# Bank order and operand spacing in the down products, and the order of work in the feed-forward norm

## The chip, the cores and the metric

The kernel runs on one core of a Trainium2 chip. The metric is the device time of one execution in microseconds. The core has five engines with a queue of instructions each, worked off in order: TensorE (PE) multiplies into eight PSUM banks, VectorE (DVE) and ScalarE (ACT) do elementwise work and can read PSUM, GpSimd (POOL) does elementwise work in SBUF and issues DMAs, SyncE (SP) issues DMAs.

## What is computed

Two decoder layers over 1024 tokens of width 1024, float32, each with a mixer, a cross-attention to 256 memory tokens and a feed-forward part. The change touches the last two.

```python
x = x + mixer(rms(x))
x = x + memory_cross_attention(rms(x), rms(mem))
x = x + swiglu(rms(x))

def swiglu(h, w_gate_up, w_down):       # hidden width 2816
    g, u = jnp.split(h @ w_gate_up, 2, axis=-1)
    return (jax.nn.silu(g) * u) @ w_down
```

## The kernel before

The residual `x` stays in SBUF, transposed: 8 blocks of 128 features, each in two halves of 512 tokens. Each float32 product is made of three matmuls (`mm3`): both operands are split in a high half (ScalarE casts, L333 for weights, L134 for operands of the down) and a low half (VectorE subtracts, L334 and L135), and high x high, high x low and low x high are accumulated.

**Seven products for eight.** The feed-forward products are done in a Winograd form: a two by two arrangement of blocks needs seven products of sums of blocks in place of eight. A product is 4 x 3 = 12 matmuls of 128 x 512. The sums of weights (s1 to s4) are made by DMAs that accumulate, issued on GpSimd's queue (L328, `add_to`), in the raw buffers `wraw` (five of them); `plan_sums` plans the loads, `pair_blocks` takes the products in a given order, splits each weight and issues the sums. `prefetch` keeps two weights split ahead of TensorE. The sums of operands (t1 to t4) are made on VectorE.

**The feed-forward loop** (`ffn`). 22 blocks of 128 hidden features. Block 0 is done plainly (`gate_up_plain`, eight products of twelve matmuls), blocks 1 to 21 by `gate_up` with seven products each, in the order of the table `ORDER`. `after` takes a product out of its bank (copies on ScalarE in `new`, L2016; adds on VectorE). `gate` scales by the norm's rows, does the Silu after a set time of the program's own clock, and scales again; `up` multiplies, and gives the hidden tile to `Down.feed`. After every even block from the second on, a down (`Down.out`) of the two blocks before takes place: seven products of four row blocks, each accumulated in a bank of its set (a, b or c, four banks each) and added to or subtracted from `x` by VectorE right after its matmuls (L193). One product's result goes into `x` in two places by letting the bank accumulate: the bank's sum is added, then the next product is put on top of it and the sum is added elsewhere. A matmul into a bank that is in use waits for the add that reads it. There are 10 downs a layer, and one in each cross-attention; the last blocks go through `outproj`.

**Operands of the down** (`Down.build`): for each chunk of two blocks, seven operands are made as soon as the hidden tiles are there: `11`, `t1`, `t2`, `21`, `t3`, `t4`, `22`, each with a cast and a low half, the four sums with a VectorE operation more. They share a number of buffers, of which a product gives its two back.

**The norm before it** (`norm_quarter`). The last products of cross-attention (`outproj`, adds at L671) come by quarters of `x`; after each, the quarter is scaled and split into operands for the gate/up products (L277, L278), squared on ScalarE (L1928) and the squares are added on GpSimd (L1932). The quarter (0, 1) makes the mixed operand t1 (L1958, L1959) and `12`, by a cast and a low half each (L1920, L1921). After the last quarter `rest` makes t2 (L1962), t3 (L1965) and t4 (L1968), and `stats` sums the squares by matmuls (`ssq`), takes the inverse root (L449 to L454) and broadcasts it (`rbp`).

**The order of work.** The program is written by generators (`Threads`) that run against a clock of the program's own, which TensorE's instructions move; a `yield` of a number lets that time pass, of an event waits for it. That fixes the order in which instructions are written down; a scheduler then lays each engine's queue in that order where operands and buffers allow. So a `yield` isn't a wait on the chip, but a place in the queues.

## Time and profile before

| | us |
|---|---|
| median of 3 runs | 2621.82 |
| lowest and highest | 2619.26, 2626.28 |
| profiled execution | 2623.92 |
| its span, first to last instruction | 2622.2 |
| TensorE busy in it | 2500.2 (95%) |
| VectorE busy in it | 1963.2 (75%) |
| ScalarE busy in it | 1079.6 (41%) |
| GpSimd busy in it | 563.0 (21%) |

The profile is of one execution. An engine's busy time is the union of its instructions' bars; a matmul's bar is longer than the interval at which matmuls follow each other, so a busy TensorE isn't one at its peak. A wait is put down to the instruction whose end released the one that waited.

### The profile page before, as it was taken

The numbers are of one execution on the slowest core, as the hardware profiler recorded it, in microseconds if no ns is written. First come the engines' busy times: TensorE is split into PE (matmuls) and PEld (weight loads), VectorE is DVE, ScalarE is ACT, GpSimd is POOL, SyncE is SP. The second block draws the span as 40 slices with busy tenths as digits, with TensorE's granted clock in tenths as the row PEclk, the third lists the DMA queues.
The fourth block names the chain that finished last, engine by engine and source line by source line (L and its number), as shares of the span: only waits on it lengthen the run. The fifth ranks groups of instructions, "written<-read, shape, count | busy, mean of one in ns | idle before, by whom it ended". The sixth has DMA issues, their size and how long they took to land. (4 is left out here: it accounts for less than half of the span.)

```text
span 2622.2 us, 34426 instructions
## 1 busy us (share of the span) xinstructions
PE 2500.2 (95%) x12029; PEld 2021.8 (77%) x12029; DVE 1963.2 (75%) x3717; ACT 1079.6 (41%) x2125; POOL 563.0 (21%) x559
## 2 busy tenths in 40 slices
PE   8999998999999999999999999999899999999998
PEld 7788886777777777779998788788677777777777
DVE  5767779877777777774637788786987777777777
ACT  5323555433333333343323377574543333333333
POOL 5311324111112111140000210032321111211122
PEclk9999999999999999999999999999999999999999
DMA  5232311455555555521122132121145555555553
GB/s 134 56 85 77 92 37 45 97 111 111 112 113 112 113 113 109 113 61 36 41 49 56 37 76 61 49 85 45 44 89 109 109 113 110 112 115 114 113 113 101
DMA packets 300093, 227.32 MB, mean 87 GB/s; under 512 B 28911, under 2 KB 250320, under 8 KB 299920
## 3 DMA queue, kind: packets, MB, share of 16 engines
q1 hardware_dynamic: 226688, 150.28, 19.7%
q0 software_dynamic: 72912, 74.32, 18.4%
q8 instruction: 94, 1.54, 0.2%
q14 instruction: 79, 0.65, 0.1%
q10 hardware_dynamic: 320, 0.53, 0.1%
HBM read 176.84 MB, written 4.19 MB: 69 GB/s over the span
## 5 line engine op out<-in xcount | busy, mean ns | idle before, releaser
L333 ACT CAST whi<-wraw 128x512 fp32r<-128x512 f32 (+1 forms) x652 | 393.0, 616 | 877.1 <-DMA wraw<-wraw 354.1
L334 DVE TENSOR_TENSOR wlo<-wraw,whi 128x512 fp32r<-128x512 f32 (+1 forms) x652 | 460.1, 716 | 223.1 <-ACT whi L333 218.5
L256 PE MATMUL dn<-fh,whi 128*128 128x512 f32 x1456 | 457.0, 401 | 36.7 <-DVE x L193 34.3
L193 DVE TENSOR_TENSOR x<-x,dn 128x512 f32<-128x512 f32 x728 | 457.3, 692 | 0.0
L256 PEld LDWEIGHTS dn<-fh,whi 128*128 128x128 f32 x1456 | 261.4, 188 | 133.6 <-DVE x L193 65.0
L256 PE MATMUL gu<-xth,whi 128*128 128x512 f32 x688 | 272.7, 396 | 18.4 <-ACT f L2016 18.4
L256 PE MATMUL dn<-fh,wlo 128*128 128x512 f32 x728 | 271.3, 394 | 0.0
L256 PE MATMUL gu<-xtl,whi 128*128 128x512 f32 x688 | 270.5, 393 | 0.0
L256 PE MATMUL gu<-xth,wlo 128*128 128x512 f32 x688 | 269.7, 392 | 0.0
L256 PE MATMUL gu<-xgh,wlo 128*128 128x512 f32 x552 | 217.0, 400 | 25.4 <-DVE wlo L334 25.3
L256 PE MATMUL pj<-xgh,whi 128*128 128x512 f32 x592 | 240.4, 406 | 0.0
L256 PE MATMUL pj<-xgh,wlo 128*128 128x512 f32 x592 | 232.6, 395 | 5.1 <-DVE wlo L334 5.1
L256 PE MATMUL pj<-xgl,whi 128*128 128x512 f32 x592 | 232.7, 393 | 0.0
L256 PE MATMUL gu<-xgh,whi 128*128 128x512 f32 x552 | 223.2, 404 | 9.4 <-DVE x L671 9.1
L256 PE MATMUL gu<-xgl,whi 128*128 128x512 f32 x552 | 219.3, 397 | 0.0
L328 POOL DMA_DIRECT2D wraw<-in_ffn_w_gate_up_dram x84 | 109.4, 1302 | 504.9 <-DVE wlo L334 210.2
L328 POOL DMA_DIRECT2D wraw<-wraw x136 | 126.6, 931 | 365.4 <-DMA wraw<-wraw 165.8
L256 PEld LDWEIGHTS gu<-xth,whi 128*128 128x128 f32 x688 | 129.1, 188 | 56.7 <-ACT f L2016 28.3
L134 ACT CAST fh<-f 128x512 fp32r<-128x512 f32 x148 | 89.5, 621 | 173.2 <-DVE f L165 69.6
L256 PEld LDWEIGHTS dn<-fh,wlo 128*128 128x128 f32 x728 | 136.7, 188 | 31.2
L256 PEld LDWEIGHTS gu<-xth,wlo 128*128 128x128 f32 x688 | 129.2, 188 | 29.3
L256 PEld LDWEIGHTS gu<-xtl,whi 128*128 128x128 f32 x688 | 129.2, 188 | 27.8
(494 smaller groups left out, 4855.5 us busy)
## 6 DMA issues: line engine op xcount, KB each, us to landing
wraw<-in_ffn_w_gate_up_dram SPq DMA_DIRECT2D x218, 256.0 KB, 2.9
wraw<-wraw POOLq DMA_DIRECT2D x136, 256.0 KB, 3.3
wraw<-in_ffn_w_down_dram SPq DMA_DIRECT2D x108, 256.0 KB, 2.7
wraw<-in_ffn_w_gate_up_dram POOLq DMA_DIRECT2D x84, 256.0 KB, 5.0
wraw<-in_od_w_in_dram SPq DMA_DIRECT2D x42, 256.0 KB, 2.8
wraw<-in_ffn_w_down_dram POOLq DMA_DIRECT2D x40, 256.0 KB, 4.2
wraw<-in_ev_w_in_dram SPq DMA_DIRECT2D x32, 256.0 KB, 2.6
wraw<-in_xattn_wkv_dram SPq DMA_DIRECT2D x32, 256.0 KB, 2.7
```

Source lines behind the costliest of these rows:

```text
L134: self.t.nc.scalar.copy(hi, src)
L193: getattr(nc.vector, op)(x, x, ps)
L256: self.nc.tensor.matmul(out, lhsT, rhs, start=start, stop=stop, skip_group_check=onto)
L328: return Step(self.th, lambda: self.nc.gpsimd.dma_start(out=raw, in_=src, accum_op=ALU.add), delay, before)
L333: self.nc.scalar.copy(hi, raw)
L334: (eng or self.nc.vector).tensor_sub(lo, raw, hi.bitcast(F32))
```

## The change

In the down products (both in the feed-forward part and in cross-attention), the order of the seven products is changed so that no two products in a row use the same banks: a, b, a, c, a, c, a. The order in which weights are loaded and summed follows the same table. Operand `22` is made before t4. In the feed-forward part a pace of 2400 ns of the program's clock is put between the making of operands, and the operands of a chunk are begun when the down before it has been written down. The unused callbacks by quarters are dropped.

In the feed-forward norm the quarter (0, 1) is split plainly like the others; the squares, their sums (now on VectorE) and the mixed operand t1 come after the last quarter, the squares first, then t1 to t4 with 1500 ns between their tiles. Block 1 of the gate/up products gets an order of its own (`first`) with s1 and s4 ahead of s2. The Silu in `gate` and in block 0 is put later by 800 and 1500 ns of the program's clock.

```diff
--- before.py
+++ after.py
@@ -119,13 +119,15 @@
 
 
 
-    FORM = (("11", "11", "a", 0, 0, 1), ("12", "21", "b", 0, 0, 1), ("s2", "t2", "a", 0, 1, 1), ("s3", "t3", "a", 1, 1, -1),
-            ("22", "t4", "a", 1, 0, -1), ("s1", "t1", "c", 1, 1, -1), ("s4", "22", "c", 0, 1, 1))
-    DONE = {"12": (0, 0), "22": (1, 0), "s1": (1, 1), "s4": (0, 1)}
-
-    def __init__(self, t, tags, eng=None, sign=1):
-        self.t, self.tags, self.eng, self.sign = t, list(tags), eng or t.nc.vector, sign
+    FORM = (("11", "11", "a", 0, 0, 1), ("12", "21", "b", 0, 0, 1), ("s2", "t2", "a", 0, 1, 1), ("s1", "t1", "c", 1, 1, -1),
+            ("s3", "t3", "a", 1, 1, -1), ("s4", "22", "c", 0, 1, 1), ("22", "t4", "a", 1, 0, -1))
+
+    def __init__(self, t, tags, eng=None, sign=1, pace=None):
+
+        self.t, self.tags, self.eng, self.sign, self.pace = t, list(tags), eng or t.nc.vector, sign, pace
         t.th.free[self] = len(self.tags)
+        self.over = {-1: Event()}
+        t.th.set(self.over[-1])
         self.full, self.right, self.ev = {}, {}, {}
 
     def parts(self, src, eng):
@@ -142,6 +144,7 @@
     def feed(self, c, i, h, tile):
         if c not in self.ev:
             self.ev[c] = {nm: Event() for nm in ("11", "21", "22", "t1", "t2", "t3", "t4")}
+            self.over[c] = Event()
             self.t.th.spawn(self.build(c))
         self.full[c, i, h] = tile
 
@@ -154,13 +157,19 @@
                 yield 500
             return self.full[c, i, h]
 
-        def operand(nm, src):
+        def operand(nm, src, fresh=True):
+            if self.pace and fresh:
+                yield self.pace / 2
             yield (self, 2)
             self.right[c, nm] = self.parts(src, self.eng)
             t.th.set(self.ev[c][nm], 2500)
+            if self.pace:
+                yield self.pace / 2 if fresh else self.pace
 
         b11 = yield from tile(0, 0)
-        yield from operand("11", b11)
+        if self.pace:
+            yield self.over[c - 1]
+        yield from operand("11", b11, False)
         b12 = yield from tile(0, 1)
         t.nc.vector.tensor_sub(b11, b11, b12)
         yield from operand("t1", b11)
@@ -168,14 +177,14 @@
         t.nc.vector.scalar_tensor_tensor(b11, b11, -1.0, b22, op0=ALU.mult, op1=ALU.subtract)
         yield from operand("t2", b11)
         b21 = yield from tile(1, 0)
-        yield from operand("21", b21)
+        yield from operand("21", b21, False)
         t.nc.vector.tensor_sub(b12, b22, b12)
         yield from operand("t3", b12)
+        yield from operand("22", b22, False)
         t.nc.vector.scalar_tensor_tensor(b11, b11, -1.0, b21, op0=ALU.mult, op1=ALU.subtract)
         yield from operand("t4", b11)
-        yield from operand("22", b22)
-
-    def out(self, c, on_quarter=None):
+
+    def out(self, c):
         t, nc, banks = self.t, self.t.nc, {}
         for w, r, to, i, h, sign in self.FORM:
             hi, lo = t.block()
@@ -194,8 +203,7 @@
                 if m % 2:
                     yield 0
             self.give(mine)
-            if on_quarter is not None and w in self.DONE:
-                on_quarter(*self.DONE[w])
+        t.th.set(self.over[c])
 
 
 class Norm:
@@ -1885,12 +1893,13 @@
         self.plan_rows(wd, (FB - 2) * P)
 
     ORDER = {"mid": (("11", "11"), ("12", "21"), ("s2", "t2"), ("s1", "t1"), ("s3", "t3"), ("s4", "22"), ("22", "t4")),
+             "first": (("11", "11"), ("12", "21"), ("s1", "t1"), ("s4", "22"), ("s2", "t2"), ("s3", "t3"), ("22", "t4")),
              "last": (("11", "11"), ("12", "21"), ("s2", "t2"), ("s1", "t1"), ("s3", "t3"), ("22", "t4"), ("s4", "22"))}
     BANK = {"11": "a", "12": "b", "s2": "a", "s1": "c", "s3": "a", "s4": "c", "22": "a"}
 
     @classmethod
     def order(cls, j):
-        return cls.ORDER["last" if j == FB - 1 else "mid"]
+        return cls.ORDER["last" if j == FB - 1 else "first" if j == 1 else "mid"]
 
     def norm_quarter(self, N, gname, off):
 
@@ -1902,51 +1911,48 @@
         N.free12 = Event()
         x, g = self.xT, [self.gain(gname, off + k) for k in range(KB)]
         ng = [self.neg[:, off + k:off + k + 1] for k in range(KB)]
-        accs, t, b12 = [[], []], [None] * 4, [None] * 4
+        accs, t, b12 = [None] * 2, [None] * 4, [None] * 4
 
         def plain(nm, i, h):
             B[nm] = []
+            tag = "g" if nm == "12" else "xg"
             for k in range(4 * i, 4 * i + 4):
-                hi, lo = self.g("xg", dt=F32R, name="xgh"), self.g("xg", dt=F32R, name="xgl")
+                hi, lo = self.g(tag, dt=F32R, name="xgh"), self.g(tag, dt=F32R, name="xgl")
                 self.split(x[h][k], hi, lo, g[k])
                 B[nm].append((hi, lo))
             th.set(N.b_ev[nm], 2000)
 
-        def mixed(nm, tag, srcs, make, eng):
+        def mixed(nm, tag, srcs, make):
             B[nm] = []
             for k in range(4):
                 make(k)
                 hi, lo = self.g(tag, dt=F32R, name="xth"), self.g(tag, dt=F32R, name="xtl")
-                nc.scalar.copy(hi, srcs[k])
-                eng.tensor_sub(lo, srcs[k], hi.bitcast(F32))
+                self.split(srcs[k], hi, lo)
                 B[nm].append((hi, lo))
-            th.set(N.b_ev[nm], 2000)
-
-        def squares(i, h, some=4):
-            for k in range(4 * i, 4 * i + 4):
-                sq = self.g("p" if k % 2 else "pt", name="sq")
-                nc.scalar.activation(sq, x[h][k], AF.Square)
-                if len(accs[h]) == 0 or k % 4 >= some:
-                    accs[h].append(sq)
-                else:
-                    nc.gpsimd.tensor_add(accs[h][0], accs[h][0], sq)
+                yield 1500
+            th.set(N.b_ev[nm], 500)
 
         def stats():
-            yield 500
-            squares(1, 1)
-            yield 4000
+            for h in range(NH):
+                for k in range(KB):
+                    sq = self.g("p", name="sq")
+                    nc.scalar.activation(sq, x[h][k], AF.Square)
+                    if k == 0:
+                        accs[h] = sq
+                    else:
+                        nc.vector.tensor_add(accs[h], accs[h], sq)
+                    yield 750
             ps = self.ps("ssq")
+            yield 1500
             self.col_sums(ps[:, 0:4], accs[0], stop=False)
-            yield 5000
             self.col_sums(ps[:, 4:8], accs[1], start=False)
-            cols = self.g("pt", (P, 3, 8), name="ncols")
+            cols = self.g("p", (P, 3, 8), name="ncols")
             v, y, tmp = (cols[:, n, :] for n in range(3))
             nc.vector.tensor_scalar(v, ps[:, 0:8], 1.0 / D, EPS, op0=ALU.mult, op1=ALU.add)
             self.rsqrt(v, y, tmp)
             for h in range(NH):
                 N.col[h] = y[:, 4 * h:4 * h + 4]
-                th.set(N.col_ev[h], 8000)
-            yield N.col_ev[0]
+            yield 5500
             for h in range(NH):
                 psb = self.bcast_cols(N.col[h], "rbp")
                 N.rb[h] = self.g("rb", name="rb")
@@ -1954,7 +1960,7 @@
                 th.set(N.rb_ev[h], 0)
 
         def t1(k):
-            b12[k], t[k] = self.g("g", name="b12"), self.g("p", name="bt")
+            b12[k], t[k] = self.g("g", name="b12"), self.g("pt", name="bt")
             nc.scalar.activation(b12[k], x[1][k], AF.Identity, scale=g[k])
             nc.vector.scalar_tensor_tensor(t[k], x[0][k], g[k], b12[k], op0=ALU.mult, op1=ALU.subtract)
 
@@ -1968,24 +1974,22 @@
             nc.vector.scalar_tensor_tensor(t[k], x[0][4 + k], ng[4 + k], t[k], op0=ALU.mult, op1=ALU.subtract)
 
         def run(i, h):
-            if (i, h) == (0, 1):
-                mixed("t1", "o", t, t1, nc.vector)
-                mixed("12", "g", b12, lambda k: None, nc.vector)
-            else:
-                plain(f"{i + 1}{h + 1}", i, h)
+            plain(f"{i + 1}{h + 1}", i, h)
             if (i, h) == (1, 1):
                 th.spawn(rest())
-                th.spawn(stats())
-                return
-            squares(i, h)
 
         def rest():
-            yield 2000
-            mixed("t2", "xg", t, t2, nc.vector)
-            yield 2500
-            mixed("t3", "g", b12, t3, nc.vector)
+            yield 1000
+            yield from stats_first()
+            yield from mixed("t1", "o", t, t1)
+            yield from mixed("t2", "xg", t, t2)
+            yield from mixed("t3", "g", b12, t3)
             yield N.free12
-            mixed("t4", "g", t, t4, nc.vector)
+            yield from mixed("t4", "g", t, t4)
+
+        def stats_first():
+            th.spawn(stats())
+            yield 12000
 
         return run
 
@@ -1993,7 +1997,7 @@
         nc, th = self.nc, self.th
         last = FB // 2 - 1
         hid, hid_ev = [[None, None], [None, None]], [Event(), Event()]
-        down = Down(self, ["pt"] * 4 + ["g"] * 4 + ["r"] * self.BUFS["r"], nc.vector, sign=-1)
+        down = Down(self, ["pt"] * 4 + ["g"] * 4 + ["r"] * self.BUFS["r"], nc.vector, -1, 2400)
 
         def hidden(j, h, t):
 
@@ -2008,7 +2012,7 @@
         def gate_up(j):
 
 
-            last = j == FB - 1
+            start, last = j == 1, j == FB - 1
             bank, t, done = {}, {}, {}
 
             def new(nm, ps):
@@ -2018,7 +2022,7 @@
             def gate(h, g):
                 yield N.rb_ev[h]
                 nc.vector.tensor_mul(g, g, N.rb[h])
-                yield 2000
+                yield 2800
                 nc.scalar.activation(g, g, AF.Silu)
                 yield 900
                 nc.vector.tensor_mul(g, g, N.rb[h])
@@ -2037,14 +2041,21 @@
                 elif w == "12":
                     nc.vector.tensor_add(t["p"], t["p"], ps)
                     th.spawn(gate(0, t["p"]))
+                elif w == "s2" and start:
+                    nc.vector.tensor_add(t["u"], t["u"], ps)
+                    th.spawn(gate(1, t["u"]))
                 elif w == "s2":
                     new("u", ps)
                 elif w == "s1":
                     new("v", ps)
                 elif w == "s3":
                     nc.vector.tensor_add(t["v"], t["v"], ps)
+                    if start:
+                        th.spawn(up(1, t["v"], t["v"]))
                     if last:
                         new("w", ps)
+                elif w == "s4" and start:
+                    new("u", ps)
                 elif w == "s4":
                     nc.vector.tensor_add(t["u"], t["u"], ps)
                     th.spawn(gate(1, t["u"]))
@@ -2075,6 +2086,7 @@
                 yield N.rb_ev[h]
                 t = self.g("p", name="f")
                 nc.vector.tensor_mul(t, gp, N.rb[h])
+                yield 1500
                 nc.scalar.activation(t, t, AF.Silu)
                 yield 1200
                 nc.vector.scalar_tensor_tensor(t, t, -1.0, up, op0=ALU.mult, op1=ALU.mult)
```

## Rows read from the trace of the kernel before

**Rows 1.** The page: the span, TensorE's busy time, and two lines of the view in 40 equal slices (tenths of busy time, tenths of full clock).

```profile
span 2622.2 us, 34426 instructions
...
PE 2500.2 (95%) x12029; PEld 2021.8 (77%) x12029; DVE 1963.2 (75%) x3717; ACT 1079.6 (41%) x2125; POOL 563.0 (21%) x559
...
PE   8999998999999999999999999999899999999998
...
PEclk9999999999999999999999999999999999999999
```

**Rows 2.** What TensorE waited for over the whole span: who waits, for whom, us in total, times, longest.

```profile
PE dn L256 <- DVE x L193: 34.3, 50, 1.7
PE gu L256 <- DVE wlo L334: 25.3, 23, 2.4
PE gu L256 <- ACT f L2016: 18.4, 23, 2.9
PE gu L256 <- DVE x L671: 9.1, 2, 4.6
```

**Rows 3.** Busy time by stretches (start:end, length, then busy us and number of instructions for PE, PEld, DVE, ACT and POOL, granted clock, DMA share, GB/s). The first two are the feed-forward layers from the first down to the last products, the other two what lies before, from the norm on.

```profile
515.30:1128.30 613.00, 580.31 (x2437) 448.93 (x2436) 465.39 (x758) 208.04 (x366) 114.80 (x113) 1.00 0.54 112
1966.75:2579.45 612.70, 580.36 (x2437) 448.81 (x2436) 465.41 (x758) 208.87 (x367) 116.19 (x115) 1.00 0.53 112
434.69:515.30 80.61, 69.86 (x289) 55.27 (x289) 68.38 (x107) 39.52 (x68) 25.74 (x22) 0.92 0.36 79
1886.20:1966.75 80.55, 69.75 (x289) 55.34 (x289) 68.30 (x106) 38.88 (x67) 25.52 (x21) 0.92 0.37 79
```

**Rows 4.** A stretch of gate/up products in the chain of work that ended last: start, length, number of matmuls.

```profile
2499.29 28.42 PE gu L256 x124
```

**Rows 5.** The same view by stretches of one cycle: a down with its tail, and the two gate/up blocks after it.

```profile
642.58:668.40 25.82, 22.75 (x92) 16.30 (x91) 24.14 (x41) 6.33 (x11) 4.35 (x4) 1.00 0.46 92
668.40:706.42 38.02, 37.20 (x162) 30.15 (x161) 23.85 (x39) 15.32 (x28) 7.85 (x8) 1.00 0.59 125
```

**Rows 6.** VectorE's order of time in that down: start, length, operation, number in a row, and in brackets the idle time before it and what ended it.

```profile
643.56 0.69 DVE L334 TENSOR_TENSOR wlo<-wraw,whi 128x512 fp32r<-128x512 f32 x1 [2.86 <-ACT whi L333]
...
646.76 1.28 DVE L193 TENSOR_TENSOR x<-x,dn 128x512 f32<-128x512 f32 x2
...
667.72 2.50 DVE L193 TENSOR_TENSOR x<-x,dn 128x512 f32<-128x512 f32 x4
```

**Rows 7.** VectorE's groups in that down, 643.5 to 668.35: busy us, mean ns, idle time before.

```profile
L135 DVE TENSOR_TENSOR fh<-f,fh 128x512 fp32r<-128x512 f32 x3 | 2.1, 694 | 0.0
```

**Rows 8.** TensorE in order of time, in the same down and at its end.

```profile
651.79 2.43 PE L256 MATMUL dn<-fh,whi 128*128 128x512 f32 x8 [0.73 <-DVE x L193]
...
655.29 0.73 PE L256 MATMUL dn<-fh,whi 128*128 128x512 f32 x2 [1.07 <-DVE x L193]
...
664.88 0.50 PE L256 MATMUL gu<-xgh,wlo 128*128 128x512 f32 x1 [1.00 <-DVE wlo L334]
```

**Rows 9.** ScalarE's copy out of a bank in the second gate/up block after it, and TensorE's matmul that waits for it.

```profile
697.40 0.57 ACT L2016 COPY f<-gu 128x512 f32<-128x512 f32 x1
...
698.02 0.50 PE L256 MATMUL gu<-xth,whi 128*128 128x512 f32 x1 [0.82 <-ACT f L2016]
```

**Rows 10.** The accumulating transfer for a gate/up weight as it is issued on GpSimd's queue, and ScalarE's cast of that weight (the first of three).

```profile
665.13 0.89 POOL L328 DMA_DIRECT2D wraw<-wraw  x1 [2.11 <-DVE wlo L334]
...
668.72 1.88 ACT L333 CAST whi<-wraw 128x512 fp32r<-128x512 f32 x3 [8.88 <-DMA wraw<-wraw]
```

**Rows 11.** Stretches at the feed-forward norm of the first layer, as in rows 3, and TensorE's first gate/up matmul there.

```profile
434.50:439.40 4.90, 0.35 (x2) 0.01 (x1) 4.90 (x5) 1.20 (x4) 3.46 (x3) 1.00 0.00 0
...
439.40:452.00 12.60, 9.95 (x27) 6.97 (x28) 12.60 (x16) 8.22 (x15) 7.90 (x6) 0.59 0.15 43
452.00:474.00 22.00, 21.04 (x99) 16.91 (x97) 22.00 (x39) 9.63 (x17) 6.66 (x6) 1.00 0.25 48
...
439.42 0.52 PE L256 MATMUL gu<-xgh,whi 128*128 128x512 f32 x1 [4.57 <-DVE x L671]
```

**Rows 12.** VectorE at that norm: low halves in order of time, then its groups from 434.5 to 477.5, and GpSimd's adds of squares from 416 to 477.5 (busy us, mean ns).

```profile
419.05 0.76 DVE L278 SCALAR_TENSOR_TENSOR xgl<-x,gains,xgh 128x512 fp32r<-128x512 f32 x1
...
420.32 1.80 DVE L278 SCALAR_TENSOR_TENSOR xgl<-x,gains,xgh 128x512 fp32r<-128x512 f32 x1
...
476.76 0.68 DVE L1921 TENSOR_TENSOR xtl<-bt,xth 128x512 fp32r<-128x512 f32 x1
...
L334 DVE TENSOR_TENSOR wlo<-wraw,whi 128x512 fp32r<-128x512 f32 x8 | 8.7, 1088 | 0.0
L278 DVE SCALAR_TENSOR_TENSOR xgl<-x,gains,xgh 128x512 fp32r<-128x512 f32 x8 | 8.2, 1024 | 0.0
L1921 DVE TENSOR_TENSOR xtl<-bt,xth 128x512 fp32r<-128x512 f32 x9 | 7.2, 802 | 0.5 <-ACT xth L1920 0.5
L1921 DVE TENSOR_TENSOR xtl<-b,xth 128x512 fp32r<-128x512 f32 x7 | 6.9, 990 | 0.0
L1962 DVE SCALAR_TENSOR_TENSOR bt<-x,neg,bt 128x512 f32<-128x512 f32 x4 | 4.0, 1000 | 0.0
...
L1932 POOL TENSOR_TENSOR sq<-sq 128x512 f32<-128x512 f32 x14 | 23.7, 1696 | 31.8 <-ACT sq L1928 31.0
```

**Rows 13.** A stretch of cross-attention with its down, as in rows 3.

```profile
390.00:402.50 12.50, 11.84 (x58) 8.99 (x57) 11.54 (x25) 8.22 (x19) 2.83 (x3) 1.00 0.06 22
```

## The prediction

> **What bounds the kernel now.** I read first the page's busy line and its forty slices: TensorE is busy 2500.2 of 2622.2 us and sits at 8 or 9 tenths nearly everywhere, at a clock of 9 tenths or more [rows 1]. So time can only come from TensorE's own gaps. Second, the list of what TensorE waited for: of about 122 us, 34.3 go to matmuls of the down products (`dn`) waiting for VectorE's residual adds (L193), 25.3 to gate/up matmuls (`gu`) waiting for a weight's low half (L334), 18.4 to `gu` waiting for ScalarE's copy out of a bank (L2016), 9.1 to two waits of 4.6 us for L671 [rows 2]. All lie in the two feed-forward layers, so third, these by stretches.
>
> Idle time understates a wait, as a matmul's bar outlasts its issue interval. 124 undisturbed matmuls of `gu` take 28.42 us, 0.229 each [rows 4]. From the first down to the last products a layer has 10 downs of 84 and 19 gate/up blocks of 84 matmuls: 2436 x 0.229 = 557.8 us, and takes 613.0 and 612.7 [rows 3]. **Excess: 55 us a layer, 5.5 us for each of 20 downs.** The stretch before it, from the norm through gate/up blocks 0 to 2, has 264 long matmuls (60.5 us) and 24 short ones, which I put at 0.1 each, 2.5: 63.0, and takes 80.6 [rows 3], **17.6 us too much, twice**. These 145 us are the most that the change can reach.
>
> In one cycle the down and its tail last 25.8 us with VectorE busy 24.1 of them, the two gate/up blocks 38.0 with VectorE busy 23.9 [rows 5]. VectorE is the limit in the down alone. Its queue there runs without a hole from the first adds on, one operation each 0.60 us (four in 2.50, the last lasting 0.70) [rows 6]. A product gives it 4 adds and one low half, 5 x 0.60 = 3.0 us, while TensorE needs 12 x 0.229 = 2.75. Also in that queue are gate operations, low halves of operands (L135, three) and one operand sum [rows 6, 7]. TensorE waits 0.73 and 1.07 us where a product returns to the bank of the product just before it [rows 8], which leaves the adds only one product's time.
>
> **The change, part by part.**
>
> *Bank order in the down.* The same 84 matmuls and 28 adds; banks go a, b, a, c, a, c, a instead of a, b, a, a, a, c, c. A bank then rests for a whole product between uses. I walk the queue from a down's start (642.6) with the first add where it is now, 646.76 or +4.2 [rows 6]: ahead of it lie a low half that waits 2.86 us for its cast, and gate operations. With 0.60 an operation and the first add of the third product done at about +12.0, the fifth product, due at 4 x 2.75 = +11.0, waits 1.0; the sixth and seventh another 0.25 each, as VectorE loses 0.25 to 0.3 a product; three restarts, which I put at 0.1 each. Sum 1.8 us. If the later Silu (2.8 instead of 2 us in the program's own time) lets adds go first and they begin 0.7 earlier, it is 0.6 or less. The planner takes the weights' order from the same table, so s1 is read fourth instead of sixth and frees its raw buffer sooner. No DMA is added: each set keeps four accumulating transfers on GpSimd's queue and five loads on SP's; the new order equals that of the gate/up blocks, which run at 0.229 in rows [rows 4]. So I cost it at nothing; without that cover a late transfer costs TensorE its own 3.6 us, from the issue to the cast (665.13 to 668.72) [rows 10].
>
> *Spacing of operands.* Building the seven operands now spreads over 2.4 us steps, and those of the next chunk wait for the end of the present down. That takes three operations (one sum, two low halves) out of the down's queue, 43 to 40, and 1.8 us of VectorE into the next gate/up block, which has 38.0 - 23.9 = 14 us to spare per two blocks [rows 5]. It also ends the bunch after the odd block, where ScalarE's copy at 697.40 came behind casts of operands and TensorE waited 0.82 [rows 9]. Nothing is queued behind a wait that didn't exist; the last operand, t4, needs buffers that the first product frees, 2.75 us into the down, and is wanted 16.5 us in. Cost zero, covered by 14 us. Behind TensorE's gate/up wait for a low half (1.00 at 664.88 [rows 8]) stood the adds; now that low half is queued before the adds of the last two products and TensorE comes first by less than 1 us, if at all.
>
> *Remainder of a cycle:* 1.8 for banks, 0.5 for what is left of the other waits and their restarts, 2.3 of 5.5. **Gain 3.2 x 20 = 64 us**; from 0.6 + 0.2 left (4.7 x 20 = 94) down to 1.5 x 20 = 30, if weights become late (first rival).
>
> *Feed-forward norm.* Before, TensorE stands still at 434.5 for 4.57 us [rows 11], since the banks it wants wait for adds that stand behind mixed operands and low halves on VectorE. The half-filled stretch after that idle time runs at a granted clock of 0.59, that is mostly at the lower of the two levels, 1.2 GHz; then the clock is back at 1.00 [rows 11]. While GpSimd adds squares (14 of 1.70 us) VectorE's low halves take 1.80 instead of 0.76, eight of them 1.02 on average [rows 12]. After, the quarter has 4 low halves in place of 12 operations, no GpSimd add runs, and TensorE should start the gate/up products almost at once: 4.6 + the next waits + the slow clock, together most of the 16.6 us that remain of 17.6 when 1.0 is left to block 2.
>
> What it adds comes later. VectorE gets 14 adds of squares (8.4 us at 0.60) and the 8 operations of t1 (5.0). Its queue is full from 434.5 to 474 [rows 11], the last low half of t4 beginning at 476.76 [rows 12], 42.9 us after the start. From this go 9.6 us of stretched time (sum over groups of the excess over 0.69 and 0.74), 7.4 that now run before the start, and 13.4 come on: 39.3. But TensorE is earlier, so 16 operations (evacuations, adds, gates, two weights) get in before: 9.6, in all 48.9. TensorE wants the last t4 tile 43 us after the start (22.0 for block 0, 2.5 short ones, 6 products and a part of block 1). So it waits about 6, with restarts and a part of t3 7.5. **Gain 9 a layer, 18**; from 16 (the 16 operations stay behind) to 4 (a second slow stretch of 12.6 us at 0.59, worth 12.6 x 0.41 = 5.2 [rows 11]). The new order of block 1 wants s4 fourth: two chained transfers within four products, hidden by block 0; a miss costs up to 3.6 once a layer. Squares on ScalarE move by 16 x 0.62; it is busy 9.6 of 22 us there [rows 11].
>
> *Cross-attention* uses the new bank order unpaced. Banks a and c stay occupied from the fourth product on, where a was freed after the fifth. TensorE there is busy 11.84 of 12.5 us [rows 13], attention being nearly through by then: between -1 and +3 us a layer; I take 0.
>
> **Sum:** 64 + 18 = 82 us off a span of 2622.2, 2540.2. The profiled execution took 2623.92 with 1.7 around its span; the median of the runs, 2621.82, is 2.1 below that. So 2540.2 + 1.7 - 2.1 = 2539.8, **2540 us**.
>
> **Rivals.** *Late weights* take the place of the bank wait. The third gate/up weight is the first one plus another, accumulated in place: its cast began 3.6 us after that issue [rows 10], then its own low half. Now it is ready about 2 us before use; with TensorE ahead, by my walk (first low half done +20.5, cast +24.4, low half done +26.4, wanted +26.6) 0.2. VectorE also carries 40 + 20 operations, 36 us, in a down and the next block of 38.4. If low halves lag 2.5 us more, 20 x 2.5 = 50 are lost: 2590, between 2568 and 2615. For it: the 2.86 us hole before a low half [rows 6]. Against it: weights precede adds in the queue.
>
> *The alternation has no effect*: c must take over b's banks, and if these are late, products four to seven wait as before. Left are the norm, 18, and about 1 us a cycle of copies: 2584. Against it: b gets the whole third product's time.
>
> *t4 comes last* (slower). Its low half is issued within the down. If it were queued behind the adds, it would end at VectorE's end, about +25.7, instead of before +18.3. TensorE would wait 7.4 a down, 4.2 more than the 3.2 gained: 2622 + 84 - 18 = 2688. It decides from some +21.5 on, when the wait eats the gain. Against it: it can start at about +5, some 13 us early.
>
> *The clock falls in the downs* (slower). Granted clock was 1.00 with all bank waits [rows 3] and 0.59 after 4.57 us of standing still. A stretch like that one, 5.2 us, in each down would add 104: 2644. Nothing in rows of downs shows it. The Trainium skill, TensorE: Matmul & The Clock Gate, section A second HAM failure mode: psum-queue depth-cycling, speaks for it: it tells of a kernel that cycled through banks each iteration, idled briefly between groups and so swung between half and full clock. By that rule shorter but more frequent holes would be worse; the trace so far disagrees, with 50 bank waits at 1.00.
>
> **Chances.** Forecast (2505 to 2568) 0.62; better still 0.05; late weights 0.17; no alternation 0.06; t4 0.06; clock 0.04. A measurement tells about 0.3%, 8 us, from no change. Of late weights 0.04 and of no alternation 0.01 fall within it. Faster 0.62 + 0.05 + 0.13 + 0.05 = 0.85, same 0.05, slower 0.10. The range 2505 to 2595 holds 0.62 + 0.11 + 0.05 = 0.78.
>
> **What would show it.** Right: waits of `dn` for L193 fall from 34.3 to under 15 us; those for L2016 under 5; a cycle of some 60 us with VectorE's busy share up to 80%; no 4.6 us hole at the norm and a clock near 1.00 there, but `gu` waits on L1921 in block 1. Wrong: `gu` waits for L334 above 25 us, or dn cycles still of 62 us or more; or a clock under 0.9 in downs.

## The result, and the profile after

The changed kernel took 2550.95 us (median of 4 runs, 2543.97 to 2555.85) beside 2622.55 for the kernel before (4 runs, 2619.26 to 2626.28): ratio 0.9725, 95% interval 0.9704 to 0.9746, faster by 71.6 us. The forecast was 2540, from 2505 to 2595.

The page of the kernel after, against [rows 1]: the span is 70.6 us shorter, TensorE has the same 12029 matmuls, and its clock stays at 9 tenths or more.

```profile
span 2551.6 us, 34493 instructions
...
PE 2475.9 (97%) x12029; PEld 2028.3 (79%) x12029; DVE 1953.1 (77%) x3745; ACT 1077.7 (42%) x2125; POOL 518.1 (20%) x531
...
PEclk9999999999999999999999999999999999999999
```

What TensorE waited for, after (who, for whom, us in total, times, longest). L2020 is the copy that was L2016, L202 the residual add that was L193, L341 and L342 the weight's cast and low half that were L333 and L334:

```profile
PE gu L264 <- ACT f L2020: 21.3, 20, 2.5
...
PE dn L264 <- DVE x L202: 5.1, 13, 0.6
PE dn L264 <- ACT whi L341: 3.4, 6, 0.6
...
PE gu L264 <- DVE f L2045: 2.6, 2, 1.4
```

Against [rows 2], the waits of the down fell from 34.3 to 5.1, those for a weight's low half (25.3) and for L671 (9.1) are gone, and those for ScalarE's copy grew from 18.4 to 21.3.

Where the time came from, by the same stretches as [rows 3] (one cycle first, then the two steady stretches, then the two norm stretches; columns as there):

```profile
627.05:687.00 59.95, 58.45 (x253) 47.16 (x253) 46.70 (x78) 21.60 (x38) 11.69 (x12) 1.00 0.57 119
502.75:1090.55 587.80, 570.56 (x2432) 454.15 (x2432) 463.44 (x758) 207.32 (x367) 115.63 (x113) 1.00 0.56 117
1922.85:2508.75 585.90, 572.33 (x2432) 451.75 (x2432) 463.22 (x758) 207.41 (x367) 116.80 (x115) 1.00 0.56 117
432.25:502.75 70.50, 66.21 (x295) 52.83 (x294) 66.35 (x118) 39.99 (x71) 9.96 (x10) 1.00 0.40 84
1849.95:1922.85 72.90, 69.25 (x295) 55.13 (x294) 66.59 (x118) 40.19 (x71) 9.96 (x10) 0.95 0.39 83
```

The steady stretches give 25.2 and 26.8, **52.0 us** (64 forecast); the norm stretches 10.1 and 7.7, **17.8** (18 forecast); the rest of the span 0.8 (0 forecast). The cycle shown is one of the best: the eight from the second to the last down of layer 0 take 486.0, 60.7 each.

What is left in a cycle, in VectorE's order of time, kernel after (start, length, idle time before and what ended it):

```profile
600.80 0.69 DVE L2060 TENSOR_TENSOR f<-f,gu 128x512 f32<-128x512 f32 x1 [1.41 <-PE gu L264]
605.88 0.69 DVE L342 TENSOR_TENSOR wlo<-wraw,whi 128x512 fp32r<-128x512 f32 x1 [4.39 <-ACT whi L341]
606.49 0.68 DVE L2024 TENSOR_TENSOR f<-f,rb 128x512 f32<-128x512 f32 x1
607.87 0.69 DVE L2028 TENSOR_TENSOR f<-f,rb 128x512 f32<-128x512 f32 x1 [0.70 <-ACT f L2026]
608.48 0.68 DVE L2035 TENSOR_TENSOR f<-gu,f 128x512 f32<-128x512 f32 x1
...
609.68 0.69 DVE L2035 TENSOR_TENSOR f<-f 128x512 f32<-128x512 f32 x1
```

And ScalarE's in the same stretch:

```profile
605.22 0.62 ACT L341 CAST whi<-wraw 128x512 fp32r<-128x512 f32 x1 [6.75 <-DMA wraw<-wraw]
607.20 0.63 ACT L2026 ACTIVATE f<-f 128x512 f32<-128x512 f32 x1 [1.36 <-DVE f L2024]
...
609.20 0.62 ACT L136 CAST fh<-f 128x512 fp32r<-128x512 f32 x1 [0.85 <-DVE f L2035]
610.39 0.62 ACT L136 CAST fh<-f 128x512 fp32r<-128x512 f32 x1 [0.58 <-DVE f L2035]
610.92 0.58 ACT L2020 COPY f<-gu 128x512 f32<-128x512 f32 x1
```

**The held-up gate.** The weight s2 is the first weight with s1 added, and s1 is itself a sum. The accumulating DMA that makes s2 is issued by GpSimd at 601.27, after 4.67 us of waiting for the one that makes s1. So ScalarE's cast is preceded by 6.75 idle us and VectorE's low half by 4.39. Behind that low half stands the gate's scaling (L2024), whose input L2060 was done at 601.5. From there everything goes in a row: Silu, scaling, hidden tiles, the operands' casts, and behind those in ScalarE's queue (at 610.92) the copy out of the bank that TensorE wants. TensorE waits 2.53 at 611.55 (row below). The same hole before a down makes its first add late, as it did in the kernel before (2.86 us [rows 6]).

### The profile page after: what moved, and what is told of

It is laid out like the page before. It is cut to its first block, busy times and chain, and to the rows that moved or that the text cites. A ratio compares the mean times of both kernels' runs of the same rounds, so it can differ in the third digit from the quotient of the medians.

```text
span 2551.6 us, 34493 instructions
## 1 busy us (share of the span) xinstructions
PE 2475.9 (97%) x12029; PEld 2028.3 (79%) x12029; DVE 1953.1 (77%) x3745; ACT 1077.7 (42%) x2125; POOL 518.1 (20%) x531
## 3 DMA queue, kind: packets, MB, share of 16 engines
q8 instruction: 95, 1.56, 0.3%
## 4 chain that ended last, share of the span: by engine, by line
PE 53%; DVE 13%; DMA 8%; issue 4%; ACT 2%; POOL 0%; DVEq 0%; ACTq 0%; POOLq 0%
PE gu L264 17%; PE dn L264 12%; PE pj L264 6%; PE tp L264 4%; PE op L264 4%; DMA wraw<-wraw 4%; DVE wlo L342 3%; DMA wraw<-in_ffn_w_gate_up_dram 3%; DVE x L202 3%; PE as L264 2%; PE ao L264 1%; PE apt L268 1%; DMA wraw<-in_ffn_w_down_dram 1%; ACT whi L341 1%; DVE f L2024 1%
## 5 line engine op out<-in xcount | busy, mean ns | idle before, releaser
L341 ACT CAST whi<-wraw 128x512 fp32r<-128x512 f32 (+1 forms) x652 | 397.5, 616 | 931.7 <-DMA wraw<-wraw 304.6
L342 DVE TENSOR_TENSOR wlo<-wraw,whi 128x512 fp32r<-128x512 f32 (+1 forms) x652 | 449.7, 695 | 198.8 <-ACT whi L341 194.0
L202 DVE TENSOR_TENSOR x<-x,dn 128x512 f32<-128x512 f32 x728 | 451.4, 676 | 0.0
L264 PEld LDWEIGHTS dn<-fh,whi 128*128 128x128 f32 x1456 | 267.4, 188 | 91.7 <-issue 19.5
L264 PE MATMUL gu<-xth,whi 128*128 128x512 f32 x672 | 268.2, 399 | 27.0 <-ACT f L2020 21.3
L264 PE MATMUL dn<-fh,wlo 128*128 128x512 f32 x728 | 285.4, 393 | 0.0
L336 POOL DMA_DIRECT2D wraw<-in_ffn_w_gate_up_dram x84 | 116.2, 1383 | 527.0 <-DVE wlo L342 255.2
L264 PE MATMUL gu<-xgh,wlo 128*128 128x512 f32 x568 | 222.2, 391 | 0.0
L264 PEld LDWEIGHTS pj<-xgh,wlo 128*128 128x128 f32 x592 | 112.2, 190 | 31.2 <-DVE wlo L342 7.2
```

Source lines behind the costliest of these rows:

```text
L202: getattr(nc.vector, op)(x, x, ps)
L264: self.nc.tensor.matmul(out, lhsT, rhs, start=start, stop=stop, skip_group_check=onto)
L336: return Step(self.th, lambda: self.nc.gpsimd.dma_start(out=raw, in_=src, accum_op=ALU.add), delay, before)
L341: self.nc.scalar.copy(hi, raw)
L342: (eng or self.nc.vector).tensor_sub(lo, raw, hi.bitcast(F32))
```

## Experiments

Each ratio is to the kernel before on the same chip. "At 2622.5" is the ratio times 2622.55, so that runs can be compared; differences between runs in us are taken from the ratios in this way.

**Parts of the change alone.** *e1_banks*: before, with the new order of banks and weights only.

```diff
-    FORM = ... s2/a, s3/a, 22/a, s1/c, s4/c
+    FORM = ... s2/a, s1/c, s3/a, s4/c, 22/a
-        (operand 22 after t4)
+        (operand 22 before t4)
```

> The kernel before with the new order of the seven down products alone (and operand 22 built before t4); no spacing of operands, nothing of the norm. Theory (banks are the main part of the cycle's gain, 5.5 us of excess a cycle to about 3): waits of dn for the residual adds fall from 34 to under 15 us and the time by 35 to 60 us, to 2563 to 2588. Rival (VectorE's queue, not the bank, sets the down, and the new order pays only together with spaced operands): waits move to gu waiting for low halves, time within 15 us of before, 2608 to 2622.

Measured 2628.56, ratio 0.999 (0.9979 to 1.0000). **Alone, the bank order gains nothing that can be told**, as the rival said, but the waits did not move to low halves. Those fell from 25.3 to 5.4 us, while the copy's grew from 18.4 to 31.5, and those of `dn` became shorter and more (kernel e1_banks, waits as above):

```profile
PE dn L256 <- DVE x L193: 42.2, 74, 0.8
PE gu L256 <- ACT f L2016: 31.5, 21, 2.9
...
PE gu L256 <- DVE wlo L334: 5.4, 4, 2.4
```

VectorE's order of time before a down of that kernel shows one reason. The hole ahead of the s2 low half is 3.59 us, and the first add comes 4.9 after the down's start (643.29), where it was 2.86 and +4.2 [rows 6]; over all 20 downs the mean of that hole goes from 2.5 to 3.4 and the mean first add from +3.8 to +4.7.

```profile
645.00 0.69 DVE L334 TENSOR_TENSOR wlo<-wraw,whi 128x512 fp32r<-128x512 f32 x1 [3.59 <-ACT whi L333]
645.61 0.68 DVE L2020 TENSOR_TENSOR f<-f,rb 128x512 f32<-128x512 f32 x1
...
648.20 1.28 DVE L193 TENSOR_TENSOR x<-x,dn 128x512 f32<-128x512 f32 x2
```

*e3_norm*: the norm part with block 1's order and block 0's later Silu, without the rest.

```diff
 (after)
-    FORM = new;  22 before t4;  Down(..., -1, 2400);  gate: yield 2800
+    FORM = old;  22 after t4;   Down(..., -1);        gate: yield 2000
```

> The kernel before with the changed feed-forward norm, the order of block 1 and the later Silu in block 0 alone; old bank order, no spacing, the old time of the gate's Silu. Theory (the norm's part stands by itself): the stretch from the norm to the first down gets 8 to 10 us shorter in each layer, the time falls by 15 to 20 us, to 2602 to 2607, and the downs keep their 34 us of waits for adds. Rival (the gain seen there came with the new bank order of cross-attention's down or with spacing in the first down): under 8 us in all, 2614 and above.

Measured 2616.62, 0.9949 (0.9932 to 0.9966), 13 us, between the two expectations. The 4.57 us hole is gone, but the stretches from the norm to the first down (433.60 to 509.14 and 1880.65 to 1954.79) got only 5.1 and 6.4 us shorter, not 8 to 10. *e2_nopace*: the whole change without gating and spacing of operands.

```diff
-        down = Down(self, [...], nc.vector, -1, 2400)
+        down = Down(self, [...], nc.vector, -1)
```

> The changed kernel with the spacing of operands taken out (no pace, and a chunk's operands may begin within the down before). Theory (spacing takes three operations out of the down's queue but leaves the wait for ScalarE's copy, which comes from a Silu held up behind a weight's low half): 5 to 15 us slower than the changed kernel, 2556 to 2566, dn waits for adds 8 to 15 us, gu waits for the copy about 20 us as with spacing. Rival (spacing carries most of the cycle's gain): 30 us or more slower, 2581 and above. Second rival (spacing costs, it makes the copy wait): faster than the changed kernel, gu waits for the copy under 15 us.

Measured 2622.29, 0.9968 (0.9958 to 0.9978). The norm and the banks are in it, and 8 us of gain are left; `dn` waits 42.5 us, the copy 27.0. That is the first rival. **So, with the new order, 64 us of the gain (0.9968 to 0.9725) hang on operands being gated or spaced.**

**What it is of these.** *e6_oldbanks*: after with the bank order of before. *e8_over*: after with a pace of 1 ns, which leaves only the rule that the next chunk's operands begin after the present down. *e4_silu*: after with the gate's Silu at its old place.

```diff
 e6: -FORM new, 22 before t4        +FORM old, 22 after t4
 e8: -Down(..., -1, 2400)           +Down(..., -1, 1)
 e4: -                yield 2800    +                yield 2000
```

> The changed kernel with the old order of the seven down products (banks a, b, a, a, a, c, c, and t4 made before operand 22) but with spacing and norm as changed. Theory (spacing shortens VectorE's queue in the down, but TensorE can run ahead of that queue only if each bank rests for a product): most of the cycle's gain is lost, 25 to 50 us slower than the changed kernel, 2577 to 2602, dn waits for adds 25 us or more. Rival (spacing alone carries the gain, as the new order alone gave none): within 12 us of the changed kernel, 2543 to 2565.

> The changed kernel with a pace of 1 ns: a chunk's operands still begin only after the down before, but they are not spaced. Theory (what pays is that three operations leave the down's queue, 1.8 us a down): within 10 us of the changed kernel, 2541 to 2562, dn waits for adds under 10 us. Rival (the steps of 2400 ns pay, as they let weights and gates pass between operands): as without spacing, 2600 and above, with copies waited for 30 us or more.

> The changed kernel with the gate's Silu back at 2000 instead of 2800 ns of the program's time. Theory (the wait of the third gate/up product for ScalarE's copy hangs on a weight that lands late and holds up VectorE and ScalarE in order, so the Silu's place matters little): within 5 us of the changed kernel, 2546 to 2556, waits for the copy 18 to 24 us. Rival (the later Silu is what holds the copy up): waits for the copy fall below 12 us and the time by 8 to 15 us, to 2536 to 2543.

Measured: e6 2574.61, 0.9784 (0.9764 to 0.9804); e8 2563.66, 0.9741 (0.9719 to 0.9762); e4 2557.85, 0.9724 (0.9706 to 0.9741). With gating the bank order is worth 0.9784 - 0.9725, 15 us; without it (e3 to e2, which also differ in the gate's Silu) it seems to cost 5, with intervals that overlap. **On the old order, gating and spacing are worth 0.9949 - 0.9784, 43 us, by themselves** (with the same difference in the Silu), so e6 lost less than its theory said and a little more than its rival. The 2.4 us steps can't be told from none, and the later Silu does nothing that can be told. The waits of e6:

```profile
PE dn L264 <- DVE x L202: 31.2, 47, 1.9
PE gu L264 <- DVE wlo L342: 11.1, 20, 1.0
...
PE gu L264 <- ACT f L2020: 1.8, 3, 1.0
```

From there to the changed kernel the waits of `dn` fall to 5.1 and those for low halves go, but the copy's grow from 1.8 to 21.3. The new order pays in the down and takes part of it back at the copy, as in e1.

**The held-up gate.** *e7_gatefirst*: after, with the second half's Silu written down at once and the cast and low half of s2 queued behind the gate.

```diff
     def split_w(...):
+        with ExitStack() as stack:
+            for ins in self.hold.pop(0) if self.hold else ():
+                stack.enter_context(self.tc.issue_after(ins))
             (cast, low half)
...
     def gate(h, g):
-        yield 2800
+        if not h: yield 2800
+        act = ...Silu
-        yield 900
+        if not h: yield 900
+        mul = ...tensor_mul
+        if h: self.hold = [(), (act.ins, mul.ins)]
```

> The changed kernel, in which the gate of the second half (two scalings on VectorE, the Silu on ScalarE) is queued ahead of the split of the summed weight s2 that follows it, on both engines, and is written down at once. Theory (that weight's sum lands late, its cast and low half stand in both queues and hold up the gate, the hidden tile, the first adds of a down and the copy that the third gate/up product waits for): gu waits for the copy fall from 21 to under 8 us, the first add of a down comes 1 us or more earlier, and the time falls by 15 to 35 us, to 2517 to 2537. Rival (the copy waits for the casts of operands that spacing puts there, or the weight becomes late instead): within 8 us of the changed kernel, 2543 to 2560, with new waits for low halves.

Measured **2506.98 (2504.99 to 2508.79), 0.9522 (0.9507 to 0.9537)**, 53 us below the change, more than the 15 to 35 expected. The copy's waits are 1.7 us in all, and `dn` waits for an add once (0.6). The edit does two things, the place in the queues and writing the Silu down at once; they were not tried apart, but 0.8 us of the Silu's place were worth nothing in e4. VectorE's order of time before a down (start 680.82), kernel e7_gatefirst:

```profile
678.25 0.69 DVE L2068 TENSOR_TENSOR f<-f,gu 128x512 f32<-128x512 f32 x1 [1.41 <-PE gu L265]
678.97 0.69 DVE L2028 TENSOR_TENSOR f<-f,rb 128x512 f32<-128x512 f32 x1
680.36 0.69 DVE L2034 TENSOR_TENSOR f<-f,rb 128x512 f32<-128x512 f32 x1 [0.70 <-ACT f L2031]
680.97 0.68 DVE L346 TENSOR_TENSOR wlo<-wraw,whi 128x512 fp32r<-128x512 f32 x1
...
682.78 2.47 DVE L202 TENSOR_TENSOR x<-x,dn 128x512 f32<-128x512 f32 x4
```

The scaling follows its input at once, the low half falls in behind without a hole, and the first add is 1.96 after the start. The cycle from there takes 57.95 us with TensorE busy throughout (stretch of that kernel, columns as in [rows 3]):

```profile
680.80:738.75 57.95, 57.95 (x253) 47.31 (x252) 47.88 (x79) 21.52 (x39) 12.44 (x13) 1.00 0.59 123
```

**Which of them is needed.** *e9_gateonly*: before with the gate first, nothing else. *e10_gate_oldbanks*: e7 with the old bank order. *e11_gate_nopace*: e7 without gating and spacing.

```diff
 e9:  before + the edit of e7 (yields 2000 and 900)
 e10: e7  -FORM new, 22 before t4   +FORM old, 22 after t4
 e11: e7  -Down(..., -1, 2400)      +Down(..., -1)
```

> The kernel before, with one thing done: the gate of a block's second half is queued ahead of the cast and low half of the summed weight s2 of the next block (its Silu is written down at once). If the held-up gate by itself costs the time of a cycle (first add about 4 us after the down's start instead of 2), the waits in the down shrink by what the first adds come earlier, about 2 us in each of 20 downs: about 2580, between 2565 and 2595. If the three operations of the next chunk in the down's queue cost as much by themselves, the queue is still 1.8 us too long and the same bank rule costs more: 2600 or more. If the hold-up matters only with the new bank order: no change, 2615 to 2625.

> The gate-first kernel (2507) with the bank order of before (a, b, a, a, a, c, c) and operand 22 after t4. If products that return at once to the same bank cost TensorE time whenever adds take longer than a product, by about 0.25 us three times a down: 2507 + 15 to 24 = 2522 to 2531, with waits of dn for L193 of over 10 us. If the alternating banks mattered only because the first adds were late: 2505 to 2512.

> The gate-first kernel (2507) without the wait of a chunk's operands for the end of the present down and without their spacing. If the three operations more in the down's queue are what the change gained by, 3 times 0.6 us come back in 20 downs, less a slack of about 0.6: 2507 + 24 to 36 = 2531 to 2543, waits of dn for L193 over 20 us. If the gating gained only since it kept the queue clear for the held-up gate, the time stays within 8 us of 2507.

Measured: e9 2561.88, 0.9727 (0.9704 to 0.9751); e10 2520.66, 0.9579 (0.9560 to 0.9597); e11 2560.14, 0.9722 (0.9698 to 0.9746). **One edit on the kernel before, e9, gives as much as the whole change**, 2551 at 2622.5, a larger gain than the 2565 to 2595 expected. The waits of e9:

```profile
PE gu L257 <- DVE wlo L338: 25.8, 24, 2.4
PE gu L257 <- DVE x L675: 9.2, 2, 4.6
PE gu L257 <- ACT f L2020: 7.5, 5, 2.9
PE dn L257 <- DVE x L193: 5.9, 11, 1.7
```

Beside [rows 2], the down's waits fall from 34.3 to 5.9 and the copy's from 18.4 to 7.5, the other two stay. e10 lies between its two expectations in time, with 3.1 us of waits of `dn` for adds and not over 10: the bank order is still worth 15 us at 2622.5 with the gate first. e11 came out 17 us above the upper end of its first expectation: without gating, 53 us are lost again. VectorE before a down of e11 (start 631.68):

```profile
633.62 0.69 DVE L346 TENSOR_TENSOR wlo<-wraw,whi 128x512 fp32r<-128x512 f32 x1 [1.71 <-ACT whi L345]
```

The gate has gone ahead, but the hidden tiles and the first add (635.43, +3.75) still stand behind this low half, whose cast waited for the accumulating DMA. The mean of this hole over the downs is 1.2 us in e11 and 0.2 in e7 and e9. So the late s2 is at work there too, one step further on.

Single downs tell what a down costs. From the trace, for one down each: the first add after the down's start, VectorE's other operations from the start to the last add, and TensorE's time over 0.229 a matmul, from the down's first to its last matmul.

```
old bank order     first add  others  excess
  before  642.59     +4.17      15     4.99
  e9      633.50     +2.27      13     2.45
  e9     1933.44     +3.80      13     4.01
  e10     741.92     +1.96      10     0.43
  e10    2434.46     +1.94      12     1.58
alternating banks
  e11     568.77     +3.52      13     2.35
  e11    2354.39     +2.57      13     1.41
  after   687.05     +2.89      11     0.49
  after  1982.41     +4.17      12     1.78
  e7      680.82     +1.95      10     0.15
```

In the old order each us that the first add is late costs TensorE one (e9: 1.53 later, 1.56 more). The rest is not all waits for banks. In the old order seven `gu` matmuls stand among those of the down, ahead of its last product, and can wait there for a weight's low half. Of e9's 2.45 at 633.50, 1.00 is this wait (653.27) and 0.23 a wait for an add. e10's second down has 1.15 more than its first, and holds the same wait of 1.00 (2453.30) and none for an add. The downs shown in the alternating order hold no `gu` matmul; e11's 1.41 at 2354.39 is one wait of 0.72 for an add and what follows it. Over all 20 downs the mean excess is 0.81 in e10, of which 0.53 lies at `gu` matmuls, and 0.18 in e7. So, with the gate first, the new order gains mostly by where these `gu` matmuls stand, and less by the rest that a bank gets; no run tries the two apart.

## Why the prediction was right, and which steps were not

**The sum was right within its range**: 2551 for 2540, in part by luck, as two of its terms missed in opposite directions.

**The excess in a cycle** was rightly read as VectorE's queue in the down. Its remainder was put at 2.3 us and came to (587.8 + 585.9 - 2 x 557.8) / 20 = 2.9; hence 52 and not 64. The down's own part was put at 1.8 with the first add at +4.2 and twelve other operations; at 1982.41, with just these, it is 1.78. Its waits there are not the 1.0, 0.25 and 0.25 of the walk, but 0.17 (1991.00) and 0.58 (1994.59); the rest is mostly longer intervals at four restarts, about 0.2 us each where I had put 0.1 for each of three. The mean of the 20 downs is about 1.2, as the first add comes at +3.3 in the mean (two of them lack five matmul records).

**The step that failed** is the 0.5 put on the other waits, with "ends the bunch" and "those for L2016 under 5". Some 1.7 a cycle (2.9 - 1.2) lie outside the downs, and the copy's waits alone are 21.3 / 20 = 1.07. The copy comes late not only because operands bunch, but because the gate behind the late s2 holds up what the operands are made from. I had the hole in [rows 6] before me and took it as the first add's offset, not as a thing to be removed; e7 removed it and 53 us. With it failed the nothing at which I had costed the new order of weights: in the old order, with gating, the copy's waits are 1.8 (e6).

**The credit was put on the wrong part.** I gave nearly all of the cycle's gain to the banks; the rival without alternation left spacing about 1 us a cycle, 20 in all. e1 (0.999) and e2 (0.9968) show that the banks alone give nothing. e3 to e6 shows that gating and spacing give 43 us without them, and e6 to the change that the banks add 15. Norm 13, gating 43 and order 15 make up the 72. e6 measures "the alternation has no effect": 2566 at 2622.5, not the 2584 of that rival. Why gating gives so much is in part open: it takes about three operations out of the down's queue, and with the new order the late weight also comes sooner (the hole before the first adds is 3.2 us in the mean in e2 and 1.9 in the changed kernel).

**Late weights**: the low halves did come late (4.39 above), but TensorE's direct waits for them, 25.3 before, are gone. That weights precede other work in VectorE's queue I used against this rival; it is just how they do their harm. The price of 2590 did not come.

**t4 last** did not happen: no wait of `dn` for the cast or the low half of an operand (`fh`) is among the waits after.

**The clock**: granted clock is 1.00 in both steady stretches after, and e1 with 74 bank waits of at most 0.8 has a mean of 0.990 beside 0.991 before. The Trainium skill (TensorE: Matmul & The Clock Gate, section A second HAM failure mode: psum-queue depth-cycling) tells of a kernel that cycled through banks and whose short idle times between groups of matmuls swung the clock between half and full; for this kernel's bank waits the trace disagrees, at 1.00. After longer holes it is another matter, below.

**The norm** came out at 17.8 for 18, and the hole of 4.57 us is gone [rows 11]. But the change to the norm by itself gives only 5.1 + 6.4 = 11.5 of these 17.8 (e3); the rest came in with the other parts, so the agreement is partly luck. Of the waits in block 1 I had named t4's; the larger ones were for adds (waits of TensorE in 432.2 to 502.8, kernel after):

```profile
PE gu L264 <- DVE f L2045: 1.4, 1, 1.4
PE gu L264 <- DVE f L2052: 0.9, 1, 0.9
PE gu L264 <- DVE xtl L283: 0.7, 2, 0.5
PE gu L264 <- ACT xth L282: 0.6, 1, 0.6
```

Layer 0 keeps 70.5 - 63.0 = 7.5 us too many, as forecast, layer 1 9.9. Of the 7.5 only 3.6 are these waits; what the rest is, I did not test. The forecast of a clock near 1.00 there held in layer 0 (1.00) and less in layer 1 (0.95). Over the whole kernel e3 puts the part at 13 us (9 to 18).

**Left open**: why s2 lands later again in e11, which has banks and norm beside e9's edit and is no faster than e9. Its first adds come at about +3.5 instead of +2, behind the low half of s2, and `dn` waits 19.3 us; what delays the transfer there was not tried.

## What to carry to other kernels

When a queue works in order, look at each hole in it for what stands behind the waiting instruction and is ready: queueing a gate's scalings and Silu ahead of a late weight's cast and low half was worth as much as this whole change, and 2% more on top of it. What a part is worth depends on the others: the bank order gave nothing alone and 15 us with gating, and gating 43 us without it, so test parts together and one by one. A stall should be traced to the transfer that started it before room is made for it.

## What was not expected of the hardware

One hole is at times followed by matmuls at the lower of the two clock levels, 1.2 GHz. TensorE in order of time after the 2.53 us wait, kernel after:

```profile
611.55 0.50 PE L264 MATMUL gu<-xth,whi 128*128 128x512 f32 x1 [2.53 <-ACT f L2020]
611.89 0.41 PE L264 MATMUL gu<-xtl,whi 128*128 128x512 f32 x1
612.12 0.60 PE L264 MATMUL gu<-xth,wlo 128*128 128x512 f32 x1
612.52 0.63 PE L264 MATMUL gu<-xth,whi 128*128 128x512 f32 x1
612.95 0.63 PE L264 MATMUL gu<-xtl,whi 128*128 128x512 f32 x1
```

Eight follow each other at about 0.43 us, with a granted clock of 0.50 from 612.20 to 615.50, then 0.23 is back: 1.6 us on top of the 2.5. In e1 a wait of 2.19 at 695.64 was followed by seven such matmuls. In e8 one of 2.67 at 615.3 was followed by none, and neither was one of 1.85 at 794.2 in the kernel after. So one wait of this size can cost more than its length; by what rule it does, these runs do not tell.
